# When the operands of the next half-size product are traced: behind the product before it, instead of behind the projection steps between them

## The chip, the cores and the metric

The kernel runs on 1 core of one Trainium2 chip. The metric is the device time of one execution in microseconds (us). Five engines work side by side, each in the order of its own queue: TensorE (PE, its weight loads PEld), VectorE (DVE), ScalarE (ACT), GpSimd (POOL) and SyncE (SP), on whose queue the large loads are issued.

## The reference

The program is two transformer blocks, one behind the other, for 512 positions of width 1024 in fp32. Each has two layers with different mixers and a two-layer network behind every mixer. Only these networks matter here:

```python
def swiglu_ffn(x, w_gate, w_up, w_down):           # first block, width 2816, layers 0 and 1
    return (jax.nn.silu(x @ w_gate) * (x @ w_up)) @ w_down
...
def sq_relu_mlp(h, w_up, w_down):                  # second block, width 4096, layers 0 and 1
    u = jax.nn.relu(h @ w_up)
    return (u * u) @ w_down
```

## The kernel before

**Precision.** Every large product is made of three matmuls (`mm3`, L178 to L182). Each operand is split into an upper half (ScalarE copies it with rounding, L152) and a lower half (VectorE subtracts, L153). L180 multiplies upper by upper, L181 uses the lower half of the moving operand, L182 the lower half of the stationary one.

**Down projection.** The hidden dimension is cut into pieces of 1024. For each piece `down_steps` (L235) multiplies a 512x1024 hidden piece by a 1024x1024 piece of the down weights with 7 half-size products instead of 8 (the scheme of Strassen and Winograd), here called p1, p2, p5, p6, p7, p3, p4 in the order in which they run. Each is 24 matmuls of 128x512. Their operands are sums and differences:

- `left` splits a 256-column part of the hidden piece, or a VectorE sum of such parts (`sum`, at L290 and L301), into a slot named `A`;
- `block` loads raw weights, 512 KB a load on SP's queue, into a pool of five slots (`rawp`);
- `chain` (from L294) holds differences of weight blocks, made by VectorE;
- `wsplit` splits weights into a pool of four slots (`wp`, names `w`).

In p5 the left operand is the sum of two hidden parts, and the right one `chain`, the difference of two weight blocks; it is the first product that needs four raw loads.

**Side steps.** Each `yield` of `down_steps` lets `weave` (L226) trace a number of steps of the next hidden piece's projection (`lin_steps`, L211), `per` at a time: two for `ffn` (L912), one for `mlp` (L1036). A step is 24 matmuls with 512 KB of weights, which go through the same raw and split pools. Behind four of them stands a chunk's evacuation: `silu` on ScalarE (L922) for the gate, a product on VectorE (L926) for the up projection, Relu on ScalarE (L1048) and a square on VectorE (L1053, or L1050 where the result is split again at once into `hidh` and `hidl`). `ffn` calls `down_steps` twice a layer, in two layers; `mlp` three times a layer, in two layers.

**What sets the order.** The kernel is traced in the order of the code. A list scheduler then gives each engine a fixed order: an instruction's rank is its place in the trace, less an offset for those traced under `high_priority` (the operands of the products, and the weights of the side steps, with 120). On the chip an engine takes its instructions in that order and waits at each until its inputs are there.

In `down_steps` before, the operands of each product are traced behind the `yield`, right ahead of the product:

```python
        product(d, us, y, True)
        out(0, 0, y)
        yield
        with early():
            tt(s1, a21, a22, ALU.add)
            d = left(s1)
            ...
        z = [self.xbank([128, 512]), self.bank([128, 512])]
        product(d, us, z, True)
```

Of the kernel before, what the change touches and what calls it, by code (L numbers as in the profile page):

```python
# [14 lines left out]
ALU = mybir.AluOpType  # L15
AX = mybir.AxisListType

ALPHA = 4.0 ** 0.25
# [54 lines left out]
class Net:  # L73
# [158 lines left out]
        for _ in side:  # L232
            pass

    def down_steps(self, h, W, k0, first, ahead=120):  # L235

        nc = self.nc
        early = lambda: self.tc.high_priority(offset=ahead)
# [5 lines left out]
        tt = nc.vector.tensor_tensor  # L248

        def left(src):  # L250
            d = self.slot([128, 2, 4, 256], F32R, "A")
            self.split(d[:, 0], d[:, 1], src)
            return d

        def block(i, j):
            return [self.raw2(W, k0 + 4 * i + k, 512 * j) for k in (0, 2)]

        def halves(t):
            return [t[:, 0:2], t[:, 2:4]]

        def product(d, us, banks, start):
            for t in range(2):
# [6 lines left out]
        def out(i, j, banks):  # L269
            for t in range(2):  # L270
                self.resid(2 * i + t, banks[t], 512 * j, first and (i, j) not in done)
            done.add((i, j))

        done = set()
        with early():
            d = left(a11)
            us = [self.wsplit(b) for b in block(0, 0)]
        x = [self.xbank([128, 512]) for _ in range(2)]
        product(d, us, x, True)
        out(0, 0, x)  # L280
        yield
        with early():
            d = left(a12)
            us = [self.wsplit(b) for b in block(1, 0)]
        y = [self.xbank([128, 512]), self.bank([128, 512])]
        product(d, us, y, True)
        out(0, 0, y)
        yield
        with early():
            tt(s1, a21, a22, ALU.add)  # L290
            d = left(s1)
            us = []
            for c, p, q in zip(halves(chain), block(0, 1), block(0, 0)):
                tt(c, p, q, ALU.subtract)  # L294
                us.append(self.wsplit(c))
        z = [self.xbank([128, 512]), self.bank([128, 512])]
        product(d, us, z, True)
        out(1, 1, z)
        yield
        with early():  # L300
            tt(s2, s1, a11, ALU.subtract)  # L301
            d = left(s2)
            us = []
            for c, p in zip(halves(chain), block(1, 1)):
                tt(c, p, c, ALU.subtract)
                us.append(self.wsplit(c))
        product(d, us, x, False)
        out(0, 1, x)
        yield
        with early():  # L310
# [6 lines left out]
        product(d, us, x, False)  # L317
        out(1, 1, x)
        yield
        with early():  # L320
            tt(a12, a12, s2, ALU.subtract)
            d = left(a12)
            us = [self.wsplit(b) for b in block(1, 1)]
        product(d, us, z, False)
        out(0, 1, z)
        yield
        with early():
# [5 lines left out]
        product(d, us, x, False)  # L333
        out(1, 0, x)
        yield

# [89 lines left out]
    def resid(self, t, ps, c0, first=False):  # L426
        r = self.r[t][:, c0:c0 + 512]
        if first:
            self.nc.vector.scalar_tensor_tensor(r, r, ALPHA, ps, ALU.mult, ALU.add)
        else:  # L430
            self.nc.vector.tensor_tensor(r, r, ps, ALU.add)  # L431

# [840 lines left out]
```

## Time and profile before

| | |
|---|---|
| Median of 3 runs | 2495.14 us (2490.13 to 2496.63) |
| The profiled execution, its own time | 2487.76 us |
| Its span in the trace | 2486.0 us |
| Mean granted clock of TensorE | 0.986 |
| TensorE busy | 2416.0 us, 97% |
| VectorE busy | 1514.2 us, 61% |
| ScalarE busy | 1026.8 us, 41% |
| Bytes moved | 291.92 MB, 117 GB/s on average |

TensorE is the bound over the whole span. The granted clock is given as a share of full speed: 1.00 is 2.4 GHz, 0.50 is 1.2 GHz. The feed-forward of layer 0 calls `down_steps` at about 529 and 662 us, that of layer 1 at about 1093 and 1225. The three calls of the first MLP begin at 1665.75, 1747.35 and 1828.95, those of the second at about 2193 us and later.

### The profile page before, as it was taken

The page shows a single profiled execution, that of the slowest core. Times are in us where ns is not written, and L with a number is a line of the kernel's source. Part 1 is how long each engine was busy: PE and PEld are TensorE (multiplying, and loading weights), DVE is VectorE, ACT ScalarE, POOL GpSimd, SP SyncE. Part 2 cuts the span into 40 slices and gives each one's busy share as a digit, 9 for nine tenths or more (in the row PEclk, how much of TensorE's full clock was granted, in tenths as well). Part 3 has the DMA queues.
Part 4 walks back from the last instruction along what each step waited for, and adds up shares of the span by engine and source line. Part 5 has one row for each costly group of instructions (what it writes and reads, how often), then busy time and mean ns, then how long its engine had stood idle before and what let it go on. Part 6 is the DMA issues. An engine that isn't in the chain of part 4 may idle for free.

```text
span 2486.0 us, 30362 instructions
## 1 busy us (share of the span) xinstructions
PE 2416.0 (97%) x12094; PEld 2012.8 (81%) x12094; DVE 1514.2 (61%) x1994; ACT 1026.8 (41%) x1620; POOL 180.0 (7%) x219
## 2 busy tenths in 40 slices
PE   8989999999999999999999999999999999999998
PEld 8877787887878997887878786888888877888887
DVE  4898666346466766446467432457876467477784
ACT  3653343223333343223334733444444456444443
POOL 1251300000000000000001002200000100000000
PEclk9999999999999999999999999999999989999999
DMA  6323122234334332235334123325543421254451
GB/s 233 110 97 107 54 94 77 88 113 165 110 129 154 127 130 76 94 102 170 110 125 149 61 85 34 102 86 185 186 161 128 152 68 36 69 170 154 151 186 68
DMA packets 148990, 291.92 MB, mean 117 GB/s; under 512 B 9449, under 2 KB 15909, under 8 KB 148592
## 3 DMA queue, kind: packets, MB, share of 16 engines
q1 hardware_dynamic: 146176, 282.17, 34.2%
q0 software_dynamic: 2096, 6.76, 1.4%
q8 instruction: 95, 1.56, 0.3%
q10 hardware_dynamic: 576, 1.05, 0.1%
q14 instruction: 47, 0.39, 0.0%
HBM read 286.77 MB, written 6.32 MB: 118 GB/s over the span
## 4 chain that ended last, share of the span: by engine, by line
PE 89%; DVE 6%; ACT 3%; issue 1%; DMA 0%; POOL 0%; SPq 0%; POOLq 0%; ACTq 0%; DVEq 0%
PE mm L180 23%; PE mm L181 23%; PE mm L182 23%; PE aux L180 5%; PE aux L182 5%; PE aux L181 5%; DVE acc L662 2%; PE aux L391 2%; DVE w L153 1%; PE aux L718 1%; PE mm L745 1%; ACT w L152 1%; PE mm L742 1%; PE aux L1195 1%; DVE bn L412 0%
## 5 line engine op out<-in xcount | busy, mean ns | idle before, releaser
L180 PE MATMUL mm<-xTh,w 128*128 128x512 f32 (+1 forms) x1696 | 614.6, 365 | 4.6 <-ACT w L152 4.1
L181 PE MATMUL mm<-xTl,w 128*128 128x512 f32 (+1 forms) x1696 | 616.7, 364 | 2.2 <-DVE xTl L153 2.2
L182 PE MATMUL mm<-xTh,w 128*128 128x512 f32 (+1 forms) x1696 | 596.0, 361 | 0.0
L153 DVE TENSOR_TENSOR w<-raw,w 128x1024 fp32r<-128x1024 f32 (+1 forms) x286 | 341.2, 1196 | 352.8 <-ACT w L152 352.4
L152 ACT ACTIVATE w<-raw 128x1024 fp32r<-128x1024 f32 (+1 forms) x286 | 293.4, 1029 | 602.6 <-PE mm L182 429.0
L180 PEld LDWEIGHTS mm<-xTh,w 128*128 128x128 f32 x1696 | 321.4, 190 | 58.0 <-ACT w L152 7.1
L181 PEld LDWEIGHTS mm<-xTl,w 128*128 128x128 f32 x1696 | 322.5, 190 | 51.4 <-DVE xTl L153 2.4
L182 PEld LDWEIGHTS mm<-xTh,w 128*128 128x128 f32 x1696 | 319.2, 189 | 48.8
L173 DVE SCALAR_TENSOR_TENSOR w<-raw,gains_T,w 128x512 fp32r<-128x512 f32 (+1 forms) x200 | 139.1, 738 | 118.1 <-ACT w L172 117.6
L172 ACT ACTIVATE w<-raw,gains_T 128x512 fp32r<-128x512 f32 (+1 forms) x200 | 131.1, 707 | 132.5 <-PE mm L182 118.5
L180 PE MATMUL aux<-w,A 128*128 128x512 f32 x440 | 172.8, 393 | 13.3 <-ACT w L152 13.3
L181 PE MATMUL aux<-w,A 128*128 128x512 f32 x440 | 172.5, 392 | 0.0
L182 PE MATMUL aux<-w,A 128*128 128x512 f32 x440 | 168.9, 391 | 0.0
L181 PE MATMUL mm<-w,xTh 128*128 128x512 f32 (+1 forms) x352 | 135.0, 383 | 0.0
L182 PE MATMUL mm<-w,xTl 128*128 128x512 f32 (+1 forms) x352 | 134.4, 384 | 0.0
L180 PE MATMUL mm<-w,xTh 128*128 128x512 f32 (+1 forms) x352 | 134.1, 384 | 0.0
L152 ACT ACTIVATE w<-chain 128x1024 fp32r<-128x1024 f32 x60 | 63.1, 1059 | 118.7 <-PE mm L182 75.0
L180 PEld LDWEIGHTS aux<-w,A 128*128 128x128 f32 x440 | 83.4, 190 | 32.3 <-ACT w L152 15.0
L181 PEld LDWEIGHTS aux<-w,A 128*128 128x128 f32 x440 | 83.6, 190 | 17.6
L182 PEld LDWEIGHTS aux<-w,A 128*128 128x128 f32 x440 | 83.4, 190 | 17.5
L431 DVE TENSOR_TENSOR r<-r,mm 128x512 f32<-128x512 f32 x76 | 51.6, 684 | 64.6 <-PE mm L182 64.5
L153 DVE TENSOR_TENSOR w<-chain,w 128x1024 fp32r<-128x1024 f32 x60 | 72.8, 1223 | 24.9 <-ACT w L152 24.6
(358 smaller groups left out, 4161.6 us busy)
## 6 DMA issues: line engine op xcount, KB each, us to landing
raw<-in_w_down SPq DMA_DIRECT2D x124, 512.0 KB, 3.3
raw<-in_ffn_wd SPq DMA_DIRECT2D x84, 512.0 KB, 3.4
raw<-in_w_up SPq DMA_DIRECT2D x64, 512.0 KB, 3.7
raw<-in_ffn_wg SPq DMA_DIRECT2D x40, 512.0 KB, 3.6
raw<-in_ffn_wu SPq DMA_DIRECT2D x40, 512.0 KB, 4.0
raw<-in_ab_w_in SPq DMA_DIRECT2D x24, 512.0 KB, 3.9
raw<-in_a_w_in SPq DMA_DIRECT2D x24, 512.0 KB, 3.5
raw<-in_xa_wk SPq DMA_DIRECT2D x16, 512.0 KB, 3.6
```

The lines of the kernel that those rows point to most:

```text
L152: self.nc.scalar.activation(hi, src, AF.Copy)
L153: self.nc.vector.tensor_tensor(lo, src, hi.bitcast(F32), ALU.subtract)
L172: nc.scalar.activation(u[:, 0, i], raw[:, i], AF.Identity, scale=g)
L173: nc.vector.scalar_tensor_tensor(u[:, 1, i], raw[:, i], g, u[:, 0, i].bitcast(F32), ALU.mult, ALU.subtract)
L180: nc.tensor.matmul(ps, lh, rh, start=start, stop=False, **kw)
L181: nc.tensor.matmul(ps, lh, rl, start=False, stop=False, **kw)
L182: nc.tensor.matmul(ps, ll, rh, start=False, stop=stop, **kw)
L391: self.nc.tensor.transpose(ps[:, j, :], src[:, j * 128:j * 128 + 128], self.ident)
L431: self.nc.vector.tensor_tensor(r, r, ps, ALU.add)
L662: nc.vector.scalar_tensor_tensor(dst, src, col, dst, ALU.mult, ALU.add)
L718: nc.tensor.matmul(d[:, h - h0, :], ke[rows, t, h * 128:h * 128 + 128], vh(t, h)[rows, :], start=True, stop=True)
L742: nc.tensor.matmul(o, P[:, h, :], vh(t, h), start=True, stop=False)
```

## The change

The operands of each product become a function (`p1`, `p2`, `p5`, ...), and the call is moved: it is traced directly behind the product before it, ahead of the `yield` and so ahead of the side steps that stand between the two products. The offset with which they are ranked goes from 120 to 60. p1's operands, which have no product of the same call before them, keep their place and get the smaller offset. `resid` gets a parameter for its operation, which is always `ALU.add`. The work is the same: no instruction is added or removed, and the matmuls of each product are the same.

```diff
-    def down_steps(self, h, W, k0, first, ahead=120):
+    def down_steps(self, h, W, k0, first, ahead=60):
...
+        def plain(i, j):
+            return [self.wsplit(b) for b in block(i, j)]
+
...
-        def product(d, us, banks, start):
+        def product(ops, banks, start):
+            d, us = ops
...
-        with early():
-            d = left(a11)
-            us = [self.wsplit(b) for b in block(0, 0)]
+        def early(f):
+            with self.tc.high_priority(offset=ahead):
+                return f()
+
         x = [self.xbank([128, 512]) for _ in range(2)]
-        product(d, us, x, True)
-        out(0, 0, x)
-        yield
-        with early():
-            d = left(a12)
-            us = [self.wsplit(b) for b in block(1, 0)]
-        y = [self.xbank([128, 512]), self.bank([128, 512])]
-        product(d, us, y, True)
-        out(0, 0, y)
-        yield
-        with early():
+
+        def p1():
+            return left(a11), plain(0, 0)
+
+        def p2():
+            return left(a12), plain(1, 0)
+
+        def p5():
             tt(s1, a21, a22, ALU.add)
             d = left(s1)
             us = []
             for c, p, q in zip(halves(chain), block(0, 1), block(0, 0)):
                 tt(c, p, q, ALU.subtract)
                 us.append(self.wsplit(c))
-        z = [self.xbank([128, 512]), self.bank([128, 512])]
-        product(d, us, z, True)
-        out(1, 1, z)
-        yield
-        with early():
+            return d, us
...
+        ops = early(p1)
+        product(ops, x, True)
+        out(0, 0, x)
+        ops = early(p2)
+        yield
+        y = [self.xbank([128, 512]), self.bank([128, 512])]
+        product(ops, y, True)
+        out(0, 0, y)
+        ops = early(p5)
+        yield
+        z = [self.xbank([128, 512]), self.bank([128, 512])]
+        product(ops, z, True)
+        out(1, 1, z)
+        ops = early(p6)
+        yield
...
```

What it does to the engines' orders differs by place. In the first `down_steps` of the first feed-forward, ScalarE's order before (`A<-sum` and `w<-chain` are splits for p5, the second `A<-sum` for p6; `sg<-mm` at L922 is the silu evacuation of a side chunk; the other splits are weights):

```order
L152 ACTIVATE w_4419<-raw_4417 128x1024
L152 ACTIVATE w_4448<-raw_4446 128x1024
L922 ACTIVATE sg_4313<-mm_4319 128x512
L922 ACTIVATE sg_4313<-mm_4320 128x512
L922 ACTIVATE sg_4313<-mm_4321 128x512
L152 ACTIVATE A_4480<-sum_4270 128x1024
L922 ACTIVATE sg_4313<-mm_4322 128x512
L152 ACTIVATE A_4590<-sum_4270 128x1024
L152 ACTIVATE w_4492<-chain_4271 128x1024
L152 ACTIVATE w_4496<-chain_4271 128x1024
```

and in the changed kernel, where the evacuation's line is L946:

```order
L152 ACTIVATE A_4313<-sg_4021 128x1024
L152 ACTIVATE A_4418<-sum_4270 128x1024
L152 ACTIVATE w_4329<-raw_4327 128x1024
L152 ACTIVATE w_4362<-raw_4360 128x1024
L152 ACTIVATE w_4430<-chain_4271 128x1024
L152 ACTIVATE w_4434<-chain_4271 128x1024
L152 ACTIVATE w_4439<-raw_4437 128x1024
L152 ACTIVATE w_4468<-raw_4466 128x1024
L152 ACTIVATE w_4536<-chain_4271 128x1024
L946 ACTIVATE sg_4326<-mm_4332 128x512
```

p5's left operand and both halves of its right one, which stood among and behind the evacuation, now stand ahead of it; so does a split of p6 (`w_4536<-chain`).

At the start of the first `down_steps` of the first MLP, TensorE's order before (`mm_12365` is a bank of a new side step, `aux<-w,A` is p1):

```order
L181 MATMUL mm_12365<-xTl_11624,w_12358 128x512
L182 MATMUL mm_12365<-xTh_11622,w_12358 128x512
L180 MATMUL mm_12365<-xTh_11622,w_12358 128x512
L181 MATMUL mm_12365<-xTl_11624,w_12358 128x512
L182 MATMUL mm_12365<-xTh_11622,w_12358 128x512
L180 MATMUL aux_12327<-w_12321,A_12314 128x512
L181 MATMUL aux_12327<-w_12321,A_12314 128x512
L180 MATMUL aux_12328<-w_12321,A_12314 128x512
L181 MATMUL aux_12328<-w_12321,A_12314 128x512
```

and in the changed kernel (`mm_12182` is the last bank of the hidden chunk that p1 multiplies):

```order
L181 MATMUL mm_12181<-xTl_11625,w_12271 128x512
L182 MATMUL mm_12181<-xTh_11623,w_12271 128x512
L180 MATMUL mm_12182<-xTh_11623,w_12271 128x512
L181 MATMUL mm_12182<-xTl_11625,w_12271 128x512
L182 MATMUL mm_12182<-xTh_11623,w_12271 128x512
L180 MATMUL aux_12314<-w_12323,A_12316 128x512
L181 MATMUL aux_12314<-w_12323,A_12316 128x512
L180 MATMUL aux_12315<-w_12323,A_12316 128x512
L181 MATMUL aux_12315<-w_12323,A_12316 128x512
L182 MATMUL aux_12314<-w_12323,A_12316 128x512
```

The 18 matmuls of the new side step that stood between the hidden chunk's last matmul and p1 stand behind p1 now.

In the third `down_steps` of that MLP, ScalarE's order before, around the evacuation of a side chunk (`tmp<-mm` is the Relu, `hidh<-tmp` the upper half of its square, `A<-h` left operands of p7, p3 and p4, in this order):

```order
L1048 ACTIVATE tmp_13784<-mm_13532 128x512
L1048 ACTIVATE tmp_13789<-mm_13533 128x512
L1048 ACTIVATE tmp_13794<-mm_13534 128x512
L152 ACTIVATE w_13893<-raw_13889 128x1024
L152 ACTIVATE hidh_13478<-tmp_13784 128x512
L152 ACTIVATE hidh_13478<-tmp_13789 128x512
L152 ACTIVATE hidh_13478<-tmp_13794 128x512
L152 ACTIVATE A_13805<-h_12938 128x1024
L152 ACTIVATE A_13886<-h_13256 128x1024
L152 ACTIVATE A_13956<-h_13256 128x1024
L1048 ACTIVATE tmp_13799<-mm_13535 128x512
```

and in the changed kernel (`A_13851` is p3's left operand, `A_13925` p4's, `w_13866` the weights of the next side step):

```order
L152 ACTIVATE w_13858<-raw_13854 128x1024
L1072 ACTIVATE tmp_13804<-mm_13545 128x512
L1072 ACTIVATE tmp_13809<-mm_13546 128x512
L1072 ACTIVATE tmp_13814<-mm_13547 128x512
L152 ACTIVATE hidh_13478<-tmp_13804 128x512
L152 ACTIVATE w_13861<-raw_13856 128x1024
L152 ACTIVATE hidh_13478<-tmp_13809 128x512
L152 ACTIVATE A_13851<-h_13270 128x1024
L152 ACTIVATE A_13925<-h_13270 128x1024
L152 ACTIVATE hidh_13478<-tmp_13814 128x512
L172 ACTIVATE w_13866<-raw_13864,gains_T 128x512 x2
L1072 ACTIVATE tmp_13819<-mm_13548 128x512
```

p7's split has gone ahead of the evacuation, and p3's and p4's stand between two `hidh`; the side step's weights stand behind them.

## Rows read from the trace of the kernel before

**Rows 1.** Engine table of the page: span; busy time and its share.

```profile
span 2486.0 us, 30362 instructions
PE 2416.0 (97%) x12094; PEld 2012.8 (81%) x12094; DVE 1514.2 (61%) x1994; ACT 1026.8 (41%) x1620; POOL 180.0 (7%) x219
```

**Rows 2.** TensorE's waits: line, waited for; us in total, times, longest.

```profile
PE aux L180 <- ACT w L152: 13.3, 4, 3.3
...
PE mm L180 <- ACT w L152: 4.1, 5, 1.1
```

**Rows 3.** Stretches: us, busy of PE, PEld, DVE, ACT, POOL; clock; DMA share; GB/s.

```profile
529.34:661.73 132.39, 128.39 (x554) 105.31 (x552) 72.26 (x72) 42.23 (x45) 0.00 (x0) 0.97 0.41 135
1665.75:1747.35 81.60, 81.60 (x362) 67.57 (x361) 62.82 (x72) 36.43 (x46) 0.00 (x0) 1.00 0.50 168
...
565.27:572.10 6.83, 5.96 (x13) 4.28 (x14) 6.83 (x7) 4.88 (x6) 0.00 (x0) 0.50 0.24 75
```

**Rows 4.** TensorE's timeline at p5: start, us, line, tiles, form, [idle before <-releaser].

```profile
565.47 0.80 PE L180 MATMUL aux<-w,A 128*128 128x512 f32 x1 [3.33 <-ACT w L152]
...
567.36 0.79 PE L180 MATMUL mm<-xTh,w 128*128 128x512 f32 x1 [0.67 <-ACT w L152]
...
568.38 0.63 PE L180 MATMUL mm<-xTh,w 128*128 128x512 f32 x1
568.81 0.63 PE L181 MATMUL mm<-xTl,w 128*128 128x512 f32 x1
```

**Rows 5.** ScalarE's timeline in the same stretch.

```profile
560.14 1.96 ACT L922 ACTIVATE sg<-mm 128x512 f32<-128x512 f32 x3 [13.22 <-PE mm L182]
562.00 1.05 ACT L152 ACTIVATE A<-sum 128x1024 fp32r<-128x1024 f32 x1
...
563.42 1.06 ACT L152 ACTIVATE A<-sum 128x1024 fp32r<-128x1024 f32 x1
564.37 2.00 ACT L152 ACTIVATE w<-chain 128x1024 fp32r<-128x1024 f32 x2
```

**Rows 6.** VectorE's timeline in the same stretch: p5's inputs.

```profile
551.91 1.22 DVE L290 TENSOR_TENSOR sum<-sg,sg 128x1024 f32<-128x1024 f32 x1
...
554.30 2.35 DVE L294 TENSOR_TENSOR chain<-raw,raw 128x1024 f32<-128x1024 f32 x2
```

**Rows 7.** Loads of the down weights: count, KB each, us to landing.

```profile
raw<-in_ffn_wd SPq DMA_DIRECT2D x84, 512.0 KB, 3.4
```

**Rows 8.** TensorE's timeline at the MLP's first p1.

```profile
1661.67 0.39 PE L180 MATMUL mm<-xTh,w 128*128 128x512 f32 x1
...
1665.75 0.39 PE L180 MATMUL aux<-w,A 128*128 128x512 f32 x1
```

**Rows 9.** ScalarE's timeline there: Relu, then p1's left operand.

```profile
1659.83 1.28 ACT L1048 ACTIVATE tmp<-mm 128x512 f32<-128x512 f32 x2 [2.06 <-PE mm L182]
1661.00 1.05 ACT L152 ACTIVATE A<-h 128x1024 fp32r<-128x1024 f32 x1
```

**Rows 10.** VectorE's timeline there: the lower half of it.

```profile
1662.09 1.23 DVE L153 TENSOR_TENSOR A<-h,A 128x1024 fp32r<-128x1024 f32 x1 [0.26 <-ACT A L152]
```

**Rows 11.** ScalarE's timeline in the third `down_steps` of the MLP.

```profile
1866.55 1.96 ACT L1048 ACTIVATE tmp<-mm 128x512 f32<-128x512 f32 x3 [2.01 <-PE mm L182]
...
1869.55 1.66 ACT L152 ACTIVATE hidh<-tmp 128x512 fp32r<-128x512 f32 x3
```

**Rows 12.** Costliest groups: the side weights' split (busy, mean ns | idle before).

```profile
L172 ACT ACTIVATE w<-raw,gains_T 128x512 fp32r<-128x512 f32 (+1 forms) x200 | 131.1, 707 | 132.5 <-PE mm L182 118.5
```

**Rows 13.** TensorE's timeline at two other short idles of the kernel.

```profile
317.10 0.39 PE L181 MATMUL mm<-xTl,w 128*128 128x256 f32 x1 [2.21 <-DVE xTl L153]
...
2026.18 0.76 PE L180 MATMUL mm<-pT,vz 128*128 128x512 f32 x1 [1.98 <-DVE ol L153]
```

**Rows 14.** The stretches behind them, columns as in rows 3.

```profile
315.00:322.00 7.00, 4.90 (x41) 4.91 (x42) 6.20 (x9) 0.00 (x0) 1.88 (x2) 1.00 0.24 75
...
2026.17:2036.41 10.24, 10.23 (x35) 7.77 (x36) 5.98 (x9) 3.86 (x11) 0.00 (x0) 0.50 0.16 53
```

More of the change, by code (lines that the diff above doesn't have):

```diff
@@ L233, in weave @@
             pass
-    def down_steps(self, h, W, k0, first, ahead=120):
+    def down_steps(self, h, W, k0, first, ahead=60):
         nc = self.nc
-        early = lambda: self.tc.high_priority(offset=ahead)
         lo, hi = slice(0, 256), slice(256, 512)
@@ L248, in down_steps @@
         tt = nc.vector.tensor_tensor
+        done = set()
         def left(src):
@@ L267, in product, with out @@
                              start and k == 0, k == 3, skip_group_check=not start)
-        def out(i, j, banks):
+        def out(i, j, banks, op=ALU.add):
             for t in range(2):
-                self.resid(2 * i + t, banks[t], 512 * j, first and (i, j) not in done)
+                self.resid(2 * i + t, banks[t], 512 * j, first and (i, j) not in done, op)
             done.add((i, j))
-        done = set()
-        with early():
-            d = left(a11)
-            us = [self.wsplit(b) for b in block(0, 0)]
+        def early(f):
+            with self.tc.high_priority(offset=ahead):
+                return f()
         x = [self.xbank([128, 512]) for _ in range(2)]
-        product(d, us, x, True)
-        out(0, 0, x)
-        yield
-        with early():
-            d = left(a12)
-            us = [self.wsplit(b) for b in block(1, 0)]
-        y = [self.xbank([128, 512]), self.bank([128, 512])]
-        product(d, us, y, True)
-        out(0, 0, y)
-        yield
-        with early():
+        def p1():
[3 more added lines that the diff above has]
+        def p5():
             tt(s1, a21, a22, ALU.add)
@@ L295, in down_steps, with p6 @@
                 us.append(self.wsplit(c))
-        z = [self.xbank([128, 512]), self.bank([128, 512])]
-        product(d, us, z, True)
-        out(1, 1, z)
-        yield
-        with early():
+            return d, us
+        def p6():
             tt(s2, s1, a11, ALU.subtract)
@@ L306, in down_steps, with p7 @@
                 us.append(self.wsplit(c))
[L307 to L310, printed above, removed]
+            return d, us
+        def p7():
             tt(a21, a11, a21, ALU.subtract)
@@ L316, in down_steps, with p3, p4 @@
                 us.append(self.wsplit(p))
[L317 to L320, printed above, removed]
+            return d, us
+        def p3():
             tt(a12, a12, s2, ALU.subtract)
[L322 to L327, printed above, removed]
+            return left(a12), plain(1, 1)
+        def p4():
             d = left(a22)
@@ L332, in down_steps @@
                 us.append(self.wsplit(c))
-        product(d, us, x, False)
+            return d, us
+        ops = early(p1)
[13 more added lines that the diff above has]
+        yield
+        product(ops, x, False)
+        out(0, 1, x)
+        ops = early(p7)
+        yield
+        product(ops, x, False)
+        out(1, 1, x)
+        ops = early(p3)
+        yield
+        product(ops, z, False)
+        out(0, 1, z)
+        ops = early(p4)
+        yield
+        product(ops, x, False)
         out(1, 0, x)
@@ L424, in ln_tile, with resid @@
         nc.vector.scalar_tensor_tensor(dst, dst, rs[:, 0:1], b, ALU.mult, ALU.add)
-    def resid(self, t, ps, c0, first=False):
+    def resid(self, t, ps, c0, first=False, op=ALU.add):
         r = self.r[t][:, c0:c0 + 512]
         if first:
-            self.nc.vector.scalar_tensor_tensor(r, r, ALPHA, ps, ALU.mult, ALU.add)
+            self.nc.vector.scalar_tensor_tensor(r, r, ALPHA, ps, ALU.mult, op)
         else:
-            self.nc.vector.tensor_tensor(r, r, ps, ALU.add)
+            self.nc.vector.tensor_tensor(r, r, ps, op)
     def hgrn_mixer(self):
```

## The prediction

> **What bounds the kernel now.** The first view is the engine table: TensorE is busy 2416.0 of 2486.0 us [rows 1], so time can only come from the 70 us in which it idles and from stretches in which it runs at the lower clock. The second is the list of what TensorE waited for. Of the waits in code that the change touches, only these two count: four waits of a product (`aux<-w,A`) on a ScalarE split, 13.3 us together and 3.3 at the longest, and five of a side step (`mm`), 4.1 us [rows 2]. Two of the four, and two of the five, lie in the first feed-forward layer, two each in the second. The third view is the table by stretches [rows 3]. The first `down_steps` of the MLP (1665.75 to 1747.35) has TensorE busy all 81.60 us at granted clock 1.00: 360 matmuls of its own, so 0.2267 us a matmul, 5.44 us a product or side step. The MLP has nothing to win. The first `down_steps` of a feed-forward layer (529.34 to 661.73) takes 132.39 us; its 7 products and 16 side steps are 552 matmuls, 552 x 0.2267 = 125.1 us. It loses 7.3 us, and there are four such calls.
>
> The fourth view is the timelines around that loss. On TensorE, product p5 starts at 565.47 after 3.33 us of waiting, the next step waits 0.67 more, and from there the matmuls follow each other by 0.43 us instead of 0.2267 [rows 4]; the stretch 565.27 to 572.10 has granted clock 0.50, that is 1.2 GHz [rows 3]. So 4.0 us of the 7.3 are the waits and 3.3 are the clock behind them. Three more places of the kernel (698, 1128 and 1261 us, p5 each time) read the same. On ScalarE the reason stands [rows 5]: it idled 13.22 us until 560.14, because the silu evacuation `sg<-mm` at the head of its queue waited for the last matmuls of the side chunk. The splits of p5's operands (`A<-sum` 562.00, `w<-chain` 564.37) stood behind it. VectorE had `sum` by 553.1 and both halves of `chain` by 556.65 [rows 6]: the operands were there, only the order held them.
>
> **What goes: p5's wait in the feed-forward.** No instruction is added or removed. In the changed order p5's splits stand on ScalarE ahead of the silu evacuation, so they run in those idle 13 us if their inputs come in time. From p1's start TensorE has p1, p2, and the side steps a and b to do before p5: 96 matmuls, 96 x 0.2267 = 21.8, so p5 is due at 529.34 + 21.8 = 551.1. The raw loads that feed `chain` stand a pair of side steps earlier in SP's queue, 2 x 5.44 = 10.9 us; VectorE's end of `chain` moves from 556.65 to about 545.8. The second split needs 1.05 us on ScalarE (564.37, two in 2.00) and 1.2 on VectorE, so about 548.1. The margin is 3 us. `sum` depends on nothing late and comes at once. The wait goes, and with no wait the clock has no reason in this trace to fall: 4 x 7.3 = 29.2 us. Bounds: if the clock drops anyway there, only the waits go, 4 x 4.0 = 16; if all goes, 29.2. I take the whole, since the MLP calls, with the same products and no wait, stay at 1.00 [rows 3].
>
> What is next to be late there? After p5 the side chunk's evacuation stands behind p5's and p6's splits on ScalarE, and those steps are still 24 matmuls (5.44 us) away from needing the bank again; TensorE's next products find their splits made under the preceding side pair. I dated p6, p7, p3 and p4 in the same way; the smallest margin is 0.4 us (the lower half of A for p3 in the second call). I book nothing; a miss of 1 us in each of four calls would stay within the range.
>
> The raw loads that move earlier take slots of the same pools (5 raw, 4 split) as the side steps' weights. SP's queue and the loads are no bound: a 512 KB load lands 3.4 us after issue [rows 7], and the DMA share over the call is 0.41 [rows 3]. VectorE and ScalarE are busy 72 and 42 of 132 us there [rows 3].
>
> **What comes: p1 without cover in the MLP.** Before, 18 matmuls of a new side step stood between the last hidden chunk and p1: they begin at 1661.67 and p1 at 1665.75 [rows 8], 4.1 us. They covered the chain from that chunk's last bank to p1's left operand: Relu from 1659.83, split `A<-h` on ScalarE 1661.00 to 1662.05 [rows 9], its lower half on VectorE 1662.09 to 1663.32 [rows 10]. In the changed order p1 stands directly behind the chunk, and the split at the same place in both queues. p1 is due at 1661.67. Its first matmuls need the upper half, 1662.05; four of them (0.9 us) fill TensorE to about 1663.0; the next kind (L182) needs the lower half, 1663.32. That is 0.4 + 0.4 = 0.8 us a call, and there are six: 4.8 us. Bounds: 0 (the scheduler's other matmuls fill it) and 1663.32 - 1661.67 = 1.65 each, 9.9 in all. I take 4.8, which is the order itself dated by the rows.
>
> **What comes: p3 in the third `down_steps` of each MLP.** There the side chunk's results are split again (`hidh`), so ScalarE has more to do at a chunk's end. Counting from 16 matmuls before the chunk's end, the first Relu starts at 1.81 and three take 1.96 [rows 11]. Behind them stand one `hidh` (0.55, three in 1.66 [rows 11]), one w split (0.95, two in 2.00 [rows 5]), one more `hidh` (0.55) and p3's `A<-h` (0.95): 6.7. p3 is due after 16 + 12 matmuls, 6.35: 0.35 late. Its four first matmuls run to 7.6; then a side step needs `w_13866`, which stands behind `A_13925`, p4's left operand (0.95), a `hidh` (0.55) and its own first half, 0.71 [rows 12]: 8.85, so 1.25 late. Together 1.6, twice: 3.2 us. Bounds: 0, if the extra splits fall into holes, and the whole A split and side weight, 2 x 3 = 6.
>
> Of the other moves (p2 to p7 in the MLP: every raw load, split and VectorE sum one side step earlier), each finds its cover: the side step of 5.44 us that stood ahead of it stands behind it now, and the smallest margin I date is 0.6 us. Nothing booked.
>
> **Sum.** -29.2 + 4.8 + 3.2 = -21.2 us. The profiled execution took 2487.76 us (span 2486.0), so it would take 2466.6. It lies 7.4 us under the median of the runs, 2495.14; the difference carried over gives 2474.
>
> A repeating gap on the engine that should be saturated is read in the Trainium skill, Perfetto Trace Analysis, section Optimization Strategy, as a possible sign that on-chip memory ran out for the next tile. What the row shows here is another cause: ScalarE idle 13.22 us and released by a TensorE bank, not by a buffer; no run so far shows a shortage, and by that reading the sum would be +8 instead of -21 (the second rival).
>
> **The rivals.** *The wait is shortened, not gone.* The raw loads of `chain` share five slots with the side weights. If one of them is issued one side step (5.44 us) later than I date it, `chain`'s second split ends at 553.5, 2.4 us after p5 is due, and the clock falls behind it as in [rows 4]; about half of each 7.3 us stays. Gain 14.6, less 8.0: -6.6, 2488. For it: each raw slot is freed by a split that stands in another queue. Against: the margin of 3 us.
>
> *The change does not do what it says: buffers, not order, hold p5.* If p5's w slots (four, shared with the side steps) come free only when the side pair is through, the splits stand earlier in the queue and still run at 562 to 566. FFN gain nil, the MLP's 8.0 us stay: 2503, slower. It decides when a w slot's last reader is a matmul of side step b. Against it: the instruction that waited 13.22 us is the silu evacuation, which takes no w slot, and the splits ran within 5 us of it with no wait of their own [rows 5].
>
> *The MLP's new waits take the clock down.* Short idles of TensorE have done both: 2.21 us at 317.10 left the clock at 1.00, 1.98 us at 2026.18 was followed by 10.24 us at 0.50 [rows 13, 14]. If all eight new waits do the latter, with 3.3 us each as behind p5, 8 x 3.3 = 26.4 is added: -21.2 + 26.4 = +5.2, 2500. Against it: the new waits are 0.4 us pieces.
>
> **How the numbers follow.** Forecast 2474, chance 0.6, its own range 2465 to 2489: it ends at the full gain with no MLP cost at all (2495.14 - 29.2 = 2466, a us off for the runs' own spread) and at the upper bounds of the two MLP costs (9.9 + 6) with a gain of 22 in the feed-forward, midway between its bounds (2495.14 - 22 + 15.9 = 2489). Shortened 0.2 (2488, 2480 to 2493), buffers 0.1 (2503), clock 0.1 (2500). The range 2465 to 2493 leaves the last two out. A measurement of this kernel tells about 0.3% (7.5 us) from no change: under 2487.6 is faster. Faster 0.7 (the forecast and half of the shortened case), same 0.2 (the other half and the clock case), slower 0.1 (the buffers case).
>
> **What would show it.** Right: the wait `aux` on ScalarE of 13.3 us gone, granted clock 1.00 and about 125 us in the first feed-forward `down_steps`; ScalarE's `w<-chain` well ahead of `sg<-mm`; in each MLP call one or two waits of 0.4 us at p1, a call of about 82.4 us; a wait of 1 us on `w` in the third. Wrong: p5 still waiting at 551 with `chain` later than 548; a clock of 0.50 behind p1 in the MLP; or a new wait at p6, p3 or p4 that I dated as covered.

## The result

The changed kernel takes 2467.47 us (median of 4 runs, 2465.86 to 2471.44), the kernel before 2493.99 us (4 runs, 2490.13 to 2496.63). The ratio is 0.9897 with a 95% interval of 0.9879 to 0.9916, so 21 to 30 us less. The forecast was 2474, from a difference of 21.2 us. The profiled execution is the longest of the four, 2471.44 us.

The page of the changed kernel, against [rows 1]: the span is 16.4 us shorter and TensorE busy 1.6 us less, so idle time is nearly all that went by these rows. The lower clock behind p5 went too (below), but its gain does not show in the busy total: other stretches ran at the lower clock for longer in this execution, and an MLP call is 0.6 us longer busy (82.20 us against 81.60).

```profile
span 2469.6 us, 30360 instructions
PE 2414.4 (98%) x12094; PEld 2010.3 (81%) x12094; DVE 1509.4 (61%) x1994; ACT 1024.4 (41%) x1620; POOL 180.5 (7%) x219
```

TensorE's waits in the first feed-forward (460 to 840 us), the whole list:

```profile
PE aux L182 <- DVE A L153: 0.7, 1, 0.7
```

and in the first MLP (1610 to 1935 us), the whole list, which was empty before:

```profile
PE aux L180 <- ACT A L152: 1.1, 4, 0.3
PE mm L180 <- ACT w L172: 0.9, 1, 0.9
```

The four waits `aux L180 <- ACT w` of [rows 2], 13.3 us, are gone, and so are the ones of the side steps behind them. In their place the MLP has eight waits of a product on its left operand, 0.3 us at the most, and two of a side step.

Two stretches of the changed kernel, in the columns of [rows 3]: the first `down_steps` of the feed-forward, from its p1 to the next call's p1, and the first of the MLP, likewise.

```profile
537.64:662.76 125.12, 125.12 (x554) 103.60 (x552) 71.22 (x72) 42.11 (x45) 0.00 (x0) 1.00 0.44 143
1643.75:1726.29 82.54, 82.20 (x361) 67.41 (x361) 62.59 (x72) 36.18 (x46) 0.00 (x0) 1.00 0.49 166
```

132.39 us have become 125.12, without an idle moment and at granted clock 1.00; 81.60 have become 82.54.

The order at p5, in the first feed-forward call of the changed kernel. ScalarE's timeline (against [rows 5]):

```profile
539.82 1.06 ACT L152 ACTIVATE A<-sum 128x1024 fp32r<-128x1024 f32 x1
...
550.18 1.06 ACT L152 ACTIVATE w<-chain 128x1024 fp32r<-128x1024 f32 x1 [5.79 <-DVE chain L296]
553.05 1.06 ACT L152 ACTIVATE w<-chain 128x1024 fp32r<-128x1024 f32 x1 [1.80 <-DVE chain L296]
...
569.35 0.60 ACT L946 ACTIVATE sg<-mm 128x512 f32<-128x512 f32 x1 [2.29 <-PE mm L182]
```

VectorE's (against [rows 6]):

```profile
551.72 1.21 DVE L296 TENSOR_TENSOR chain<-raw,raw 128x1024 f32<-128x1024 f32 x1
...
553.45 2.35 DVE L153 TENSOR_TENSOR w<-chain,w 128x1024 fp32r<-128x1024 f32 x2
```

and TensorE's, where p5 starts with no idle time ahead of it (against [rows 4]):

```profile
559.40 0.39 PE L180 MATMUL aux<-w,A 128*128 128x512 f32 x1
```

All of p5's splits are done by 555.80 (553.45 + 2.35), 3.6 us ahead of p5 and 13.5 us ahead of the silu evacuation that they stood behind before.

TensorE's order in this call changed as well. In the kernel before, a pair of side steps (48 matmuls) stood between p1 and p2 and another between p2 and p5, so p5 stood 144 matmuls behind p1's first. In the changed kernel p2 follows p1 directly, 4 of p5's 24 matmuls are mixed into the side steps from the 96th on (559.40 is the first of them), and the other 20 stand from the 148th on:

```profile
571.19 0.39 PE L180 MATMUL aux<-w,A 128*128 128x512 f32 x1
```

### The profile page after: what moved, and what is told of

It reads as the page before. It is cut to its first block, busy times and chain, and to the rows that moved or that the text cites. A ratio compares the mean times of both kernels' runs of the same rounds, so it can differ in the third digit from the quotient of the medians.

```text
span 2469.6 us, 30360 instructions
## 1 busy us (share of the span) xinstructions
PE 2414.4 (98%) x12094; PEld 2010.3 (81%) x12094; DVE 1509.4 (61%) x1994; ACT 1024.4 (41%) x1620; POOL 180.5 (7%) x219
## 3 DMA queue, kind: packets, MB, share of 16 engines
q10 hardware_dynamic: 576, 1.05, 0.1%
## 4 chain that ended last, share of the span: by engine, by line
PE 88%; DVE 7%; ACT 2%; issue 1%; DMA 1%; POOL 0%; SPq 0%; POOLq 0%; DVEq 0%; ACTq 0%
PE mm L180 23%; PE mm L181 23%; PE mm L182 23%; PE aux L182 5%; PE aux L180 4%; PE aux L181 4%; DVE acc L686 2%; PE aux L415 2%; PE aux L742 1%; DVE w L153 1%; PE mm L769 1%; PE mm L766 1%; PE aux L1219 0%; DVE bn L436 0%; ACT A L152 0%
## 5 line engine op out<-in xcount | busy, mean ns | idle before, releaser
L180 PE MATMUL mm<-xTh,w 128*128 128x512 f32 (+1 forms) x1696 | 611.4, 363 | 2.8 <-ACT w L172 1.8
L182 PE MATMUL mm<-xTh,w 128*128 128x512 f32 (+1 forms) x1696 | 574.0, 362 | 0.0
L180 PEld LDWEIGHTS mm<-xTh,w 128*128 128x128 f32 x1696 | 320.5, 190 | 53.2 <-ACT w L172 2.6
L173 DVE SCALAR_TENSOR_TENSOR w<-raw,gains_T,w 128x512 fp32r<-128x512 f32 (+1 forms) x200 | 140.7, 736 | 122.1 <-ACT w L172 121.6
L180 PE MATMUL aux<-w,A 128*128 128x512 f32 x440 | 169.6, 391 | 2.1 <-ACT A L152 2.1
L180 PE MATMUL mm<-w,xTh 128*128 128x512 f32 (+1 forms) x352 | 134.6, 385 | 0.0
L180 PEld LDWEIGHTS aux<-w,A 128*128 128x128 f32 x440 | 82.6, 188 | 22.7 <-ACT A L152 5.8
L153 DVE TENSOR_TENSOR xTl<-aux,xTh 128x512 fp32r<-128x512 f32 x72 | 47.3, 682 | 60.1 <-ACT xTh L152 60.1
```

Of the source, the lines that this page charges most:

```text
L153: self.nc.vector.tensor_tensor(lo, src, hi.bitcast(F32), ALU.subtract)
L173: nc.vector.scalar_tensor_tensor(u[:, 1, i], raw[:, i], g, u[:, 0, i].bitcast(F32), ALU.mult, ALU.subtract)
L180: nc.tensor.matmul(ps, lh, rh, start=start, stop=False, **kw)
L182: nc.tensor.matmul(ps, ll, rh, start=False, stop=stop, **kw)
```

## The experiments

All variants come from one form of `down_steps`. A product that is named in `late` gets its operands in the old place, behind the `yield` and with the old offset; the others stand in the new place.

```diff
-    def down_steps(self, h, W, k0, first, ahead=60):
+    def down_steps(self, h, W, k0, first, ahead=60, late=(), far=120, first_ahead=None):
...
-        def early(f):
-            with self.tc.high_priority(offset=ahead):
+        def early(f, by=None):
+            if f.__name__ in late:
+                return f
+            with self.tc.high_priority(offset=by or ahead):
                 return f()
+
+        def need(f):
+            with self.tc.high_priority(offset=far):
+                while callable(f):
+                    f = f()
+            return f
...
         ops = early(p5)
         yield
+        ops = need(ops)
         z = [self.xbank([128, 512]), self.bank([128, 512])]
```

`first_ahead` is not used in any run. `ALL` below stands for the names of all seven products. With all seven late and the offset 60 instead of 120, every engine's order in the program is that of the kernel before, row for row; with all seven in the new place and the offset 120 it is that of the changed kernel. The offset does nothing here; the place is the whole change.

**How the runs are read.** The runs of one kernel spread by up to 14 us, and much of that is TensorE's clock. In [rows 4] matmuls follow each other by 0.43 us at half the clock, where 0.2267 is usual, so a run's time multiplied by its mean granted clock is about the time that it would take at full clock. Over the 17 runs of the kernel before in the first set, time has a standard deviation of 4.2 us and the product 1.4; in the other two sets it is 4.7 and 2.3, and 4.5 and 2.7. The product is no sure gain: the clock is given to three places (0.001 is 2.5 us), and over the five or six runs each of again, ffn_only and p5_only the product spreads more than the time (3.9, 3.3 and 3.5 us against 3.0, 2.0 and 1.7). Differences of 2 or 3 us in it are not safe. The length of a region in the traces, at granted clock 1.00, is the finer measure, and it is given where it decides. The table has both time and product; the kernel before has 2490.25 us and 2452.9 in the first set (of again, ffn_only, mlp_only, p5_only), 2491.53 and 2453.4 in the second (the next four), 2489.71 and 2453.7 in the third.

| | median us | ratio to before, 95% | mean clock | mean of time x clock |
|---|---|---|---|---|
| again: the changed kernel | 2471.30 | 0.9919 (0.9901 to 0.9937) | 0.9893 | 2444.7 |
| ffn_only | 2459.07 | 0.9875 (0.9857 to 0.9894) | 0.9908 | 2437.5 |
| mlp_only | 2491.95 | 1.0008 (0.9995 to 1.0021) | 0.9870 | 2460.2 |
| p5_only | 2457.85 | 0.9870 (0.9852 to 0.9888) | 0.9900 | 2434.2 |
| mlp_p2_late | 2477.83 | 0.9945 (0.9932 to 0.9959) | 0.9908 | 2455.7 |
| p5_left_late | 2489.66 | 0.9993 (0.9980 to 1.0005) | 0.9883 | 2460.9 |
| p5_chain_late | 2475.88 | 0.9936 (0.9919 to 0.9953) | 0.9890 | 2448.8 |
| old_wp5 | 2540.48 | 1.0196 (1.0180 to 1.0211) | 0.9732 | 2472.8 |
| mlp0_new | 2490.74 | 1.0005 (0.9991 to 1.0020) | 0.9866 | 2456.6 |
| mlp1_new | 2496.74 | 1.0017 (1.0003 to 1.0031) | 0.9842 | 2456.2 |

**again.** No edit.

> The changed kernel once more, beside the kernel before. Theory A (the sum of the prediction is complete): the difference is the 21 us that the two traces show in the touched calls, so about 2472 if the kernel before takes 2493. Theory B (the first runs' 26.5 us is right and the sum lacks some 5 us, outside the touched calls or in runs whose clock falls more often): 2466 to 2468.

2471.3 against 2490.25, 19 us less, with an interval of 16 to 25. That is theory A: its 21 us lies in both intervals, theory B's 26.5 not in the second. The product falls by 8.2, that is 16 us of waits less 8; the mean clock rises from 0.9847 to 0.9893, and 0.0046 x 2490 = 11.5 us is the clock's part.

**ffn_only and mlp_only.** The one has all seven late in `mlp`, the other in `ffn`:

```diff
-            self.weave(self.down_steps(h, a["w_down_2"][l], 8 * b - 8, False), hidden(b, more, out), 1)
+            self.weave(self.down_steps(h, a["w_down_2"][l], 8 * b - 8, False, late=ALL), hidden(b, more, out), 1)
```

> The four feed-forward calls in the new place, the six MLP calls in the old one. Theory (both regions add up, the MLP part is a loss of 7.7 us in the trace): 7 to 8 us faster than the changed kernel, about 2460; no wait of a product on ScalarE in either region. Rival (the MLP's short waits cost nothing at the end, something else stands beside them): the same as the changed kernel, 2467.

> The six MLP calls in the new place, the four feed-forward calls in the old one. Theory: the feed-forward waits are all there again (13.3 us on a ScalarE split, granted clock 0.50 behind each), and the MLP adds its 7.7 us: about 8 us slower than the kernel before, 2501 to 2503. Rival (the MLP's new order brings something that its calls hide): the same as before, 2493 to 2495.

With the feed-forward alone the time is 12.2 us under the changed kernel of the same set, more than the 7 to 8 expected, and the product 7.2. No product waits on ScalarE; p3 waits 0.72 us on VectorE in one call. The MLP's part is a loss. How large it is, the traces tell without the clock of other stages. From TensorE's last instruction of the stage before the first MLP to its first of the stage behind it, in the columns of [rows 3], for the kernel before and the changed one:

```profile
1622.62:1932.31 309.69, 309.58 (x1434) 258.88 (x1433) 217.56 (x255) 135.52 (x176) 1.98 (x5) 1.00 0.45 150
...
1604.27:1918.03 313.76, 311.64 (x1434) 258.33 (x1433) 217.12 (x255) 134.65 (x176) 1.97 (x5) 1.00 0.43 148
```

So the first MLP is 4.07 us longer with the operands of all seven products in the new place; mlp_only has the same 313.75, and ffn_only, with the old place, 309.77. The second is 4.03 us longer, read likewise up to TensorE's last instruction. That is 8.1 us for the two. With the MLP alone the product rises by 7.3 us, as the theory has it, but the time only by 1.7 (interval -1 to +5): a miss in time. The difference is the clock, 0.9870 against 0.9847, 5.7 us. In the profiles it does not lie at p5, where both have 6.8 us at 0.50 in all four calls, but in stretches whose code no edit here touches. Two of them, 20 to 450 us (ahead of every `down_steps`) and 1980 to 2130 us (the sliding-window stage, which the changed kernel reaches some 14 us earlier), in the columns of [rows 3], for the kernel before:

```profile
20.00:450.00 430.00, 409.44 (x2346) 343.38 (x2345) 317.06 (x448) 180.47 (x308) 89.78 (x83) 0.98 0.30 99
1980.00:2130.00 150.00, 139.68 (x676) 109.84 (x675) 96.32 (x210) 85.52 (x241) 3.75 (x6) 0.92 0.21 70
```

for mlp_only:

```profile
20.00:450.00 430.00, 408.62 (x2348) 341.55 (x2348) 317.23 (x448) 180.74 (x306) 89.14 (x83) 0.99 0.30 99
1980.00:2130.00 150.00, 143.44 (x705) 112.21 (x704) 99.29 (x215) 88.40 (x246) 3.75 (x6) 0.95 0.26 84
```

and for the changed kernel:

```profile
20.00:450.00 430.00, 410.96 (x2297) 343.02 (x2296) 314.02 (x444) 179.47 (x306) 89.48 (x81) 0.96 0.29 96
1980.00:2130.00 150.00, 141.27 (x727) 112.89 (x728) 98.57 (x213) 91.13 (x250) 4.45 (x10) 0.95 0.15 50
```

The first stretch runs the same order in all three and has a clock of 0.98, 0.99 and 0.96: 0.03 of 430 us is about 13 us from nothing that an edit here changed. Over all the profiled executions but old_wp5's, this stretch goes from 0.96 to 0.99. The second does not run the same order in all three: the list scheduler has put this stage's instructions in another order too, though its code is the same. In the programs only mlp1_new has the order of the kernel before there; mlp_only and mlp0_new share a second, ffn_only and p5_only a third, and the changed kernel has a fourth, near the first. So a difference of the clock there can be the order's or the execution's, and no run here parts the two.

**mlp0_new and mlp1_new.** Only the first MLP (`l == 0`), or only the second, in the new place:

```diff
-8 * b - 8, False), hidden(b, more, out), 1)
+8 * b - 8, False, late=ALL if l == 1 else ()), hidden(b, more, out), 1)
```

> Only the first MLP's three calls in the new place, everything else in the old one. Both theories: 3.9 us more of waits in that MLP, so time times clock 3.9 us over the kernel before (2453 to 2457). Theory A (the small cost in time with both MLPs in the new place came from the sliding-window stage behind the first MLP, which lost less clock because it was reached at another moment): granted clock 0.002 over the kernel before and no more time than it, -2 to +1 us. Theory B (that was the spread of the clock in the untouched stretches, which no edit of the MLP moves): clock as before and +4 us.

> Only the second MLP's three calls in the new place. Both theories: 3.9 us more of waits, time times clock 2457 against 2453. Theory A and theory B alike: nothing behind the second MLP can win, so the clock as before and +4 us; a gain of clock here too would speak against theory A.

Each has its own MLP's waits and none in the other. In mlp0_new the first MLP's region takes 313.74 us, in mlp1_new, where it stands in the old place, 309.76. The products rise by 2.9 and 2.5 us, less than the 3.9, but within what the product can tell. In time the first costs 1.0 us (interval -2 to +5) and the second 7.0 (1 to 8). The first is what theory A expects; but the second's clock fell by 0.0011, where both theories had no change, about as much as the first's rose (0.0013). What moves the clock by chance is as large as what theory A rests on. There is a rival that neither theory names: mlp0_new and mlp_only, whose clock rose, have another order in the sliding-window stage, and mlp1_new, whose clock did not, has the old one. Whether the later start of that stage, its order or chance saved the clock stays open.

**p5_only.** In the feed-forward `late` holds all but p5, in the MLP all.

> Only p5's operands in the feed-forward in the new place; every other product in both regions in the old one. Theory (p5's splits behind the silu evacuation are the whole loss): all of the gain and none of the cost, 2493 - 29 = 2464 at the most, rather 2460, as with the feed-forward alone. Rival (the wait moves on to p6, p3 or p4, which need the new place too): a new wait of a product there, and at least 5 us more than with the feed-forward alone.

It has all of the gain: 2457.85 us, 32 under the kernel before and 13 under the changed kernel of the same set; ffn_only's 2459.07 is not told apart from it. Between them these two are the fastest versions. No product waits in either region, and the feed-forward's first 125 us have TensorE busy throughout:

```profile
536.00:661.00 125.00, 125.00 (x553) 103.52 (x552) 72.12 (x72) 42.10 (x46) 0.00 (x0) 1.00 0.44 143
```

The six other moves bring nothing that these runs can tell, and the rival (the wait moves on to p6, p3 or p4) falls. TensorE's order changed here too: half of p5's matmuls follow p2 directly. So p5_only alone doesn't say that ScalarE's order held p5. The two variants with one operand late do, since in both TensorE has p5 144 matmuls behind p1 as before.

**old_wp5.** The order of the kernel before (all late), and

```diff
-        self.wp = pool("wp", 4)
+        self.wp = pool("wp", 5)
...
-        self.big = pool("big", 15)
+        self.big = pool("big", 14)
```

> The order of the kernel before with five slots for split weights instead of four, and 14 large slots instead of 15 to make room. Theory (order, not buffers, holds p5): the splits of p5 still stand behind the silu evacuation, the four waits of 3.33 us stay, 2488 to 2495. Rival (four slots are too few for p5's two and the side steps' weights): the four waits go or shrink by half or more, 2462 to 2478.

The time is far off the forecast: with one large slot less TensorE waits 52.45 us once, ahead of 200 us and far from any `down_steps`. The order elsewhere differs with it, so the verdict rests on p5's place alone. ScalarE's timeline there:

```profile
606.26 1.96 ACT L960 ACTIVATE sg<-mm 128x512 f32<-128x512 f32 x3 [18.61 <-PE mm L182]
608.12 1.05 ACT L152 ACTIVATE A<-sum 128x1024 fp32r<-128x1024 f32 x1
...
610.49 2.00 ACT L152 ACTIVATE w<-chain 128x1024 fp32r<-128x1024 f32 x2
```

and TensorE's:

```profile
611.60 0.80 PE L180 MATMUL aux<-w,A 128*128 128x512 f32 x1 [3.33 <-ACT w L152]
```

The same order around p5 and the same 3.33 us as in [rows 4, 5], at all four places, although ScalarE now idles 18.6 us ahead of it. A fifth slot changes nothing: the split slots did not hold p5. The raw slots were not varied, but p5_only loses the wait with the same five, so they did not hold it either.

**p5_chain_late and p5_left_late.** p5_only, but of p5 only one operand in the new place. The first:

```diff
         def p5():
             tt(s1, a21, a22, ALU.add)
             d = left(s1)
-            us = []
-            for c, p, q in zip(halves(chain), block(0, 1), block(0, 0)):
-                tt(c, p, q, ALU.subtract)
-                us.append(self.wsplit(c))
-            return d, us
+            def rest():
+                us = []
+                for c, p, q in zip(halves(chain), block(0, 1), block(0, 0)):
+                    tt(c, p, q, ALU.subtract)
+                    us.append(self.wsplit(c))
+                return d, us
+            return rest
```

The second has the chain's loop ahead of `rest` and the sum and `left(s1)` in it.

> As p5 alone in the new place, but of its operands only the sum and the left split; the chain's loads, differences and splits stay in the old place. In ScalarE's order the first chain split stands behind three silu evacuations and three A splits. Theory (the order on ScalarE is what holds p5, so both operands must pass the evacuation): p5 waits 3 to 4 us in each of four calls, the clock falls, and the time is that of the kernel before, 2486 to 2494. Rival (the left operand alone held p5): 2458 to 2463.

> As p5 alone in the new place, but of its operands only the chain and its splits; the sum and the split of the left operand stay in the old place, so in ScalarE's order they stand behind three of the silu evacuations, and nothing of p5 behind them. Theory: ScalarE frees from the third silu as p5 is due and needs one split (1.05 us); p5 waits 0.9 to 1.3 us in each of four calls instead of 3.33. If a wait of this size leaves the clock at 1.00, 2458 + 4 x 1.2 = 2463; if the clock falls behind it as behind 3.33 us, 2458 + 4 x 4.5 = 2476. Rival (the left operand has other cover): no wait at all, 2458.

p5_chain_late gave 2475.88, neither theory's number. ScalarE's timeline in the first call:

```profile
561.56 0.60 ACT L963 ACTIVATE sg<-mm 128x512 f32<-128x512 f32 x1 [13.22 <-PE mm L182]
...
565.85 1.06 ACT L152 ACTIVATE w<-chain 128x1024 fp32r<-128x1024 f32 x1
```

and in the second:

```profile
693.61 0.60 ACT L963 ACTIVATE sg<-mm 128x512 f32<-128x512 f32 x1 [13.22 <-PE mm L182]
...
696.00 1.07 ACT L152 ACTIVATE w<-chain 128x1024 fp32r<-128x1024 f32 x1
```

The chain's split comes 4.3 us behind the first silu in one call and 2.4 in the other, and p5 waits 3.4 and 1.51 us, in both layers alike; in three of the four calls its second matmul waits 0.53 us more. The expectation was read from the first call's order alone. The mechanism stands: a split behind the evacuation costs the time by which it is late, and both operands have to pass it.

p5_left_late has p5 waiting on its left operand for 0.95 us at four places, as the theory says. But two more things came with it. TensorE's timeline:

```profile
565.44 2.08 PE L182 MATMUL mm<-xTh,w 128*128 128x512 f32 x4 [3.98 <-DVE w L153]
...
578.32 0.50 PE L180 MATMUL aux<-w,A 128*128 128x512 f32 x1 [0.95 <-ACT A L152]
```

and VectorE's:

```profile
563.03 1.23 DVE L315 TENSOR_TENSOR chain<-raw,chain 128x1024 f32<-128x1024 f32 x1 [1.82 <-DMA raw<-in_ffn_wd]
564.17 1.22 DVE L153 TENSOR_TENSOR w<-raw,w 128x1024 fp32r<-128x1024 f32 x1
```

A side step waited 2.07 to 3.98 us in each call for the lower half of its weights, which stood in VectorE's queue behind a chain difference whose raw load had not landed. And in the MLP, where the edit also put the chain ahead of the sum, each of the six calls got a wait of 1.1 to 1.3 us on VectorE. So the time says nothing on the theory; the 0.95 us do. They stand against 3.33 us at the same place in TensorE's order: with the chain's splits ahead of the evacuation and only the left one behind, most of the wait is gone.

**mlp_p2_late.** The changed kernel with `late=("p2",)` in `mlp`.

> The changed kernel, but in the MLP's six calls p2's operands stand in the old place. Its order then has 18 matmuls of the side step ahead of p1 again, and in the third call 15 ahead of p3. Theory (the MLP's cost is that p2's weights take the split that the next side step had, so p1 and p3 lose their cover): the four waits of 0.28 us on A in each MLP and the 0.9 us on w go, time times clock falls by 7 to 8 us, 2460 to 2464. Rival (every product's move costs its part in the MLP): only some of the eight waits go, and 3 us or more of the cost stay, 2467 to 2471.

Half of it held. p1's waits are gone, all six, with the side step ahead of it again, and so is p3's own wait; of the 0.89 us on `w` 0.46 and 0.49 are left. But the time is a miss, 2477.83 against 2460 to 2464: the ratio is worse than the changed kernel's (0.9945 against 0.9919), and the product 11 us higher. TensorE's timeline in the first MLP call:

```profile
1645.86 0.39 PE L180 MATMUL aux<-w,A 128*128 128x512 f32 x1
...
1656.40 0.51 PE L180 MATMUL mm<-xTh,w 128*128 128x512 f32 x1 [0.41 <-ACT w L172]
...
1662.56 0.73 PE L182 MATMUL mm<-xTh,w 128*128 128x512 f32 x2 [1.74 <-DVE w L173]
```

and VectorE's:

```profile
1659.48 2.36 DVE L153 TENSOR_TENSOR w<-chain,w 128x1024 fp32r<-128x1024 f32 x2
1661.75 1.41 DVE L173 SCALAR_TENSOR_TENSOR w<-raw,gains_T,w 128x512 fp32r<-128x512 f32 x2
```

With p2 one step later and p5 where it was, the operands of both fall into one step; VectorE works through them without a gap, and the next side step's weights (`L173`) stand behind p5's. Each call gets a wait of 1.74 to 1.77 us for them, and one of 0.41 us ahead of it. So p2's operands (the run moves its left operand and its weights together) are what takes p1's cover, and moving p2 alone back is no cure. Other mixtures were not run; what is shown to be free of the loss is the whole old order in the MLP, as in ffn_only.

## Why the prediction was right, by its own steps

**What bounds the kernel.** The order on ScalarE held p5. This is shown by p5_only (the whole gain from p5's operands), old_wp5 (no gain from a slot) and the pair with one operand late, in which TensorE's order at p5 is the old one and the wait follows the split that stands behind the evacuation.

**p5 dated.** Due 21.8 us after p1: it started at 559.40, 21.76 after 537.64. `chain` complete 16.5 us after p1: it was at 552.93 (551.72 + 1.21), 15.3 after. Margin 3 us: 3.6. Only 4 of p5's 24 matmuls stand so early; the other 20 come at 571.19, so for most of p5 the margin was 15 us (571.19 - 555.80), not 3. The first call won 7.27 us of the 7.3 that it lost.

**The margins booked at nothing.** One of them was thin and came out: p3 in the second call of the first layer, dated with 0.4 us to spare, waits 0.70 us for the lower half of its left operand, behind the `hidl` of the evacuation in VectorE's queue. In the second layer it does not. The same wait, 0.71 or 0.72 us, is in again, ffn_only and mlp_p2_late, and not in p5_only: it is the price of the moves beside p5.

**p1 in the MLP.** The forecast for a call was 0.8 us. TensorE's timeline:

```profile
1643.08 0.39 PE L182 MATMUL mm<-xTh,w 128*128 128x512 f32 x1
1643.75 0.50 PE L180 MATMUL aux<-w,A 128*128 128x512 f32 x1 [0.28 <-ACT A L152]
...
1644.55 0.40 PE L181 MATMUL aux<-w,A 128*128 128x512 f32 x1
1645.01 0.49 PE L182 MATMUL aux<-w,A 128*128 128x512 f32 x1
```

The first matmul comes 0.67 us behind the last one instead of 0.23, and the first that needs the lower half 0.46 behind its forerunner: 0.44 + 0.23 = 0.67, the rest in slightly longer steps between. The call is 0.94 us longer (82.54 - 81.60), and the second is too. Mis-sized by 0.14 a call, 0.8 in all. It is shown that the lost cover is p2's doing (mlp_p2_late).

**p3 in the third call.** The forecast was 1.6 us. TensorE's timeline:

```profile
1858.08 0.39 PE L182 MATMUL aux<-w,A 128*128 128x512 f32 x1
1858.69 0.50 PE L180 MATMUL aux<-w,A 128*128 128x512 f32 x1 [0.23 <-ACT A L152]
...
1859.49 0.39 PE L181 MATMUL mm<-w,A 128*128 128x512 f32 x1
1860.77 0.50 PE L180 MATMUL mm<-xTh,w 128*128 128x512 f32 x1 [0.89 <-ACT w L172]
```

0.23 and 0.89, behind the instructions that the prediction names, on ScalarE:

```profile
1857.59 2.00 ACT L152 ACTIVATE A<-h 128x1024 fp32r<-128x1024 f32 x2
1859.48 0.62 ACT L152 ACTIVATE hidh<-tmp 128x512 fp32r<-128x512 f32 x1
1860.01 1.32 ACT L172 ACTIVATE w<-raw,gains_T 128x512 fp32r<-128x512 f32 x2
```

These idle times count from the end of the matmul before, as the profile models it. From start to start, as the prediction counts, the two matmuls come 0.38 us (1858.69 - 1858.08, less 0.23) and 1.05 us (1860.77 - 1859.49, less 0.23) late, 1.4 together. By the MLP's length the price is 4.07 - 3 x 0.94 = 1.25. So the forecast was 0.2 to 0.35 too high; the three Relu took 1.73 us in this execution, not the 1.96 of [rows 11]. The prediction's own terms, as it gives them, add up to 6.77 and 8.98, not 6.7 and 8.85, which would have put it about 0.1 higher still.

**The sum.** The first feed-forward's region, from TensorE's last instruction of the stage before it to its first of the stage behind it, in the columns of [rows 3], before and in the changed kernel:

```profile
448.57:794.89 346.32, 337.90 (x1526) 280.57 (x1524) 183.12 (x189) 112.14 (x130) 3.21 (x4) 0.98 0.40 131
...
456.87:789.58 332.71, 332.00 (x1525) 276.91 (x1524) 182.29 (x191) 112.20 (x130) 4.27 (x5) 1.00 0.42 136
```

It won 13.61 us, and the second layer's 14.54 (350.09 against 335.55): 28.2, where 29.2 was forecast. The two MLPs lost 8.1, where 8.0 was forecast. So the touched regions won 20.1 us, against 21.2. In part this is luck: p1's price was set 0.8 us too low over the six calls and p3's some 0.5 too high over the two, which nearly cancel. The interval of again (16 to 25) holds the 20.1, that of the first runs (21 to 30) begins just above it, and 26.5, the first difference, was some 6 us more than the touched regions explain. What the prediction did not see is how little one profiled execution says on the rest: the two profiled executions differ by 16.3 us, not 20. In the two stretches shown above, whose code is untouched, the changed kernel had 0.96 of the clock where the kernel before had 0.98 (0.02 x 430 = 8.6 us lost), and 0.95 where it had 0.92 (0.03 x 150 = 4.5 us back).

**The rivals.** The wait was not shortened but gone. The buffers were no bound: old_wp5 has the same 3.33 us with a split slot more, and p5_only has no wait with the slots as they were. The Trainium skill (Perfetto Trace Analysis, section Optimization Strategy) says that a repeating gap can mean too little on-chip memory; these two runs speak against that at p5. The MLP's eight waits of 0.3 and two of 0.9 us left the clock alone: 1.00 over the first MLP's 313.76 us, with both kinds in it.

## What to carry to other kernels

An in-order engine that idles 13 us behind one waiting instruction holds back everything queued behind it: date when those inputs were ready, and move only the operands that are late. Here one product of seven needed the new place, in one of the two regions that call the code. In the other region no operand was late, and the same edit cost 8 us there, because operands that moved ahead took the places that had given another step its cover. Read the same edit apart for each region that calls it. A list scheduler can reorder a stage whose code the edit does not touch, so compare the orders there before calling it unchanged. When the clock moves in such stretches, compare the length of the touched region in the traces; time multiplied by the granted clock helps only as far as its own spread allows.

## What was not expected of the hardware

The price of an idle moment of TensorE beyond its own length. In the touched calls of all these profiles, idles of up to 1.31 us, where no longer one stood just ahead, were not followed by the lower clock; six of 1.74 to 1.77 us in mlp_p2_late were not, either. Two of 1.51 us in p5_chain_late, each with 0.53 us more about 1 us later, went both ways, the first with 1.00 behind it, the second with a stretch at 0.50. Idles of 2.07 us and more were all followed by one (outside these calls the 2.21 us of [rows 13] were not). Rows of p5_chain_late behind its two idles of 1.51 us, in the columns of [rows 3]:

```profile
696.00:706.00 10.00, 8.35 (x35) 6.61 (x36) 9.10 (x10) 5.89 (x8) 0.00 (x0) 1.00 0.38 121
...
1256.13:1259.55 3.42, 3.42 (x10) 2.66 (x9) 3.42 (x4) 1.67 (x2) 0.00 (x0) 0.50 0.07 8
```

and of p5_left_late behind idles of 3.98 and 2.85 us:

```profile
564.08:570.90 6.82, 5.46 (x13) 4.31 (x14) 3.04 (x4) 0.00 (x0) 0.00 (x0) 0.50 0.69 231
697.20:700.61 3.41, 2.96 (x7) 2.38 (x8) 2.13 (x3) 0.00 (x0) 0.00 (x0) 0.50 0.86 260
```

The lower clock lasted 6.8 us in one case and 3.4 in the other, so such a wait costs another 3.4 us or about half of that. The prediction's 3.3 us behind each of p5's waits were read from one execution, but they hold: of the 20 waits of 3.33 us at p5 in the five profiled executions that have them, 19 were followed by 6.8 us at 0.50 and one, in old_wp5, by 3.4 us. The 3.40 us waits in p5_chain_late had 6.8 us behind it in the first layer and 3.4 in the second. What decides between the two lengths, and between a fall and none, these runs do not show.
